# Ten of the 22 column pairs of an FFN's input stage computed as seven block products instead of eight

## The chip, the cores and the metric

The kernel runs on one core of a Trainium2 chip. The core has five engines that work side by side, each through its own queue in order: TensorE (PE in the profile, its weight loads as PEld), VectorE (DVE), ScalarE (ACT), GpSimd (POOL) and SyncE (SP, here a queue for DMAs). They meet by semaphores. The metric is the time of one execution on the device in microseconds (us).

## The reference

One decoder layer over 512 tokens of 1024 channels, in float32. The first half (input projection, attention, pooling mixer, gates, output projection, layer norm) gives `h`. The change concerns the first matrix product of the second half, with `D_FF` = 2816:

```python
a, u = jnp.split(h @ w_ffn_in[l], 2, axis=-1)
a = causal_dwconv(a, conv_w[l], conv_b[l])
f = (jax.nn.gelu(a, approximate=False) * u) @ w_ffn_out[l]
h = layer_norm(ALPHA * h + f, ln2_g[l], ln2_b[l])
```

`w_ffn_in` is 1024 x 5632. The convolution is causal along the tokens, of width 3, channel by channel.

## The kernel before

**Three matmuls for one.** Every float32 operand is split into a high part, rounded to the format fp32r, and a low part, the rest. `split` makes both: ScalarE copies the source into the high part (line 67), VectorE subtracts it from the source (line 68). `mm3` (lines 144 to 148) then issues three matmuls into the same PSUM bank: high x high, high x low, low x high.

**Weights.** `chunks` lists all weight tiles (128 x 1024, 512 KB) in the order of their use. `weights(i)` hands out tile i and has `fetch` load the next ones, up to LEAD = 3 ahead: a DMA on SP's queue into one of three `wraw` buffers, then the split into one of RING = 5 pairs of `whi` and `wlo` buffers. A buffer is filled again when its last reader is done.

**The FFN's input stage.** The 5632 columns are 44 tiles of 128, in 22 pairs: tile 2f is the gate path `a` and tile 2f + 1 the path `u` of the same 128 channels. `hT_hi` and `hT_lo` hold the transposed `h` (8 slices of 128 channels, 512 tokens); `ln1_T` makes them from four token blocks by transposes on TensorE. `fi_mm(j, b, t)` (line 575) computes tile j into a PSUM bank: 8 slices times three matmuls over the tokens `t`. The first five tiles run in two halves of 256 tokens, because the last token blocks come late; the rest run over all 512. After each pair `gated` (line 580) takes the `a` bank through the convolution (one ScalarE and two VectorE instructions), the gelu (ScalarE), and multiplies it with the `u` bank into `fT` (VectorE).

**The output stage** is already a product of 2 x 2 blocks by seven products (`product`, `operands`). Its weight sums are made by DMAs: `tw` is loaded on SP's queue and added to by an accumulating DMA on POOL's queue (lines 641 and 642 for the first product, T3, and line 134 for the later ones). Its token-side operands are differences of `fT`, made by `formed` (line 607) at fixed pairs of the input stage.

**Order.** The program is written stage by stage, and a planner (the tile framework with its schedule on) then decides where each instruction stands in its engine's queue and which free buffer a tile gets. So the loops give what depends on what, and the order on each engine is read from the built program.

Of the kernel before, what the change touches and what calls it, by code (L numbers as in the profile page):

```python
# [22 lines left out]
NF = DFF // P  # L23
# [9 lines left out]
RING = 5  # L33
# [3 lines left out]
NLATE = 4  # L37
KH = NF // 2
TAIL = 8
PRODUCTS = ("T3", "B11", "B21", "T1", "T2", "B22", "T4")  # L40


@with_exitstack
def layer_kernel(ctx: ExitStack, tc: tile.TileContext, xT, x, w_v, w_c, rel_bias, invcnt, w_group,
                 pscale, w_br, w_out, lnr, w_fi, convp, w_fo, out):
    nc = tc.nc
    const = ctx.enter_context(tc.tile_pool(name="const", bufs=1))
    wp = ctx.enter_context(tc.tile_pool(name="wp", bufs=1))
# [7 lines left out]
    def bank(name):  # L56
        return ps.tile([P, S], F32, tag="ps", name=name)
# [5 lines left out]
    def split(hi, lo, src, copy=None):  # L63
        if copy:
            copy(hi, src)
        else:
            nc.scalar.activation(hi, src, AF.Copy)  # L67
        nc.vector.tensor_tensor(lo, src, hi.bitcast(F32), op=ALU.subtract)  # L68
# [9 lines left out]
    chunks = [w_v[c] for c in range(4)]  # L78
# [4 lines left out]
    WO0 = len(chunks)  # L83
    chunks += [w_out[k * P:(k + 1) * P, :] for k in range(KT)]
    FI0 = len(chunks)
    chunks += [w_fi[j] for j in range(2 * NF)]
    FO0 = len(chunks)
    chunks += [(p, c) for p in PRODUCTS for c in range((KH + 1) // 2)]
    ready = {}
    state = {"next": 0, "limit": WO0 - 1}  # L90

    def fetch(pool=None, early=None):
        i = state["next"]
        state["next"] = i + 1
        if isinstance(chunks[i], tuple):
            ready[i] = fetch_fo(i, *chunks[i])
            return
        raw = wp.tile([P, D], F32, tag="wraw", name=f"wraw{i}", bufs=3)
        if pool is None:
            hi = wp.tile([P, D], F32R, tag="whi", name=f"whi{i}", bufs=RING)  # L100
            lo = wp.tile([P, D], F32R, tag="wlo", name=f"wlo{i}", bufs=RING)
        else:
            hi = pool.tile([P, D], F32R, name=f"whi{i}")
            lo = pool.tile([P, D], F32R, name=f"wlo{i}")
        parts = 2 if early else 1
        for c in range(parts):
            sl = slice(c * (D // parts), (c + 1) * (D // parts))
            (nc.scalar if early else nc.sync).dma_start(raw[:, sl], chunks[i][:, sl])
            split(hi[:, sl], lo[:, sl], raw[:, sl], fast if early and c == 0 else None)
            if c == 0 and early:  # L110
                early()
        ready[i] = (hi, lo)

    def half(name, sl):
# [24 lines left out]
    def weights(i):  # L139
        while state["next"] <= min(i + LEAD, state["limit"]):  # L140
            fetch()
        return ready[i]

    def mm3(out_, w, a, start, stop, **kw):
        (wh, wl), (ah, al) = w, a
        nc.tensor.matmul(out_, wh, ah, start=start, stop=False, **kw)  # L146
        nc.tensor.matmul(out_, wh, al, start=False, stop=False, **kw)  # L147
        nc.tensor.matmul(out_, wl, ah, start=False, stop=stop, **kw)  # L148

    def split3(v, a):  # L150
        return tuple(t.rearrange("p (a c) -> p a c", a=a) for t in v)
# [275 lines left out]
    for f in range(KT):  # L427
        if f == KT - LEAD:
            state["limit"] = WO0 + RING - 1
        wh, wl = split3(weights(BR0 + f), KT)  # L430
# [4 lines left out]
        for br in (1, 0):  # L435
            b = bank(f"br{f}_{br}")
# [3 lines left out]
            t = bp.tile([P, S], F32, tag="m", name=f"m{f}_{br}", bufs=4)  # L440
# [19 lines left out]
    lnb = ln_rows(0)  # L460
# [3 lines left out]
    hTp = hp.enter_context(tc.tile_pool(name="hTp", bufs=1, reuse_waits="tile"))  # L464
    hT_hi = hTp.tile([P, KT, S], F32R, name="hT_hi")
    hT_lo = hTp.tile([P, KT, S], F32R, name="hT_lo")
    st = const.tile([P, NT, 4, 6], F32, name="st")
    mv = const.tile([P, NT, 2], F32, name="mv")
    rstd = const.tile([P, NT, 2], F32, name="rstd")
# [67 lines left out]
    def ln1_T(i):  # L537
        for n in range(2):
            b = bank(f"ht{i}_{n}")
            for k in range(4):  # L540
                kt = 4 * n + k
                nc.tensor.transpose(b[:, k * P:(k + 1) * P], xs[:, i, kt * P:(kt + 1) * P], ident)
            split(hT_hi[:, 4 * n:4 * n + 4, i * P:(i + 1) * P], hT_lo[:, 4 * n:4 * n + 4, i * P:(i + 1) * P],
                  b.rearrange("p (a c) -> p a c", a=4))

    def wo_mm(wb, i, k):
        wh, wl = ready[WO0 + k]
# [25 lines left out]
    ln1_vec(3, wb[3])  # L573

    def fi_mm(j, b, t):
        wh, wl = split3(weights(FI0 + j), KT)
# [3 lines left out]
    def gated(j, a, u):  # L580
        y = ytiles[j % 2]
        nc.scalar.activation(y, a, AF.Identity, bias=cvp[:, j, 3:4], scale=cvp[:, j, 2:3])
        nc.vector.scalar_tensor_tensor(y[:, 1:], a[:, :S - 1], cvp[:, j, 1:2], y[:, 1:], op0=ALU.mult, op1=ALU.add)
        nc.vector.scalar_tensor_tensor(y[:, 2:], a[:, :S - 2], cvp[:, j, 0:1], y[:, 2:], op0=ALU.mult, op1=ALU.add)  # L584
        nc.scalar.activation(y, y, AF.Gelu)  # L585
        nc.vector.tensor_tensor(fT[:, j, :], y, u, op=ALU.mult)  # L586

    actp.close()
    fw = ctx.enter_context(tc.tile_pool(name="fw", bufs=1, side="right", reuse_waits="tile"))
    fT = fw.tile([P, NF, S], F32, name="fT")  # L590
    tw = fw.tile([P, KH * S], F32, name="tw")
    sd = [tuple(fw.tile([P, KH, 256], F32R, name=f"sd0_{q}") for q in ("hi", "lo"))]
    rb = fw.tile([P, 3, 256], F32, name="rb")
    NC = (KH + 1) // 2
    cuts = [slice(k, min(k + 4, KH)) for k in range(0, KH, 4)]
    t1, t2 = slice(0, 256), slice(256, 512)
# [10 lines left out]
    def formed(j):  # L607
        for c in cuts:
            if j == c.stop - 1:
                nc.vector.tensor_tensor(rd(c), side(0, c, t1), side(0, c, t2), op=ALU.subtract)  # L610
                side_split(0, c, rd(c))
            if j == KH + c.stop - 1:
                nc.vector.tensor_tensor(side(0, c, t2), side(1, c, t2), side(0, c, t2), op=ALU.subtract)
                nc.vector.scalar_tensor_tensor(rd(c), side(1, c, t2), -1.0, rd(c),
                                               op0=ALU.mult, op1=ALU.subtract)

    hb = {}
    for j in range(RING):
        hb[j] = bank(f"fi{j}")
        fi_mm(j, hb[j], slice(0, 256))  # L620
        if j == 0:
            ln1_T(2)
        elif j == RING - 2:
            ln1_T(3)
    for j in range(RING):
        state["limit"] = FI0 + RING + j
        fi_mm(j, hb[j], slice(256, 512))
        if j % 2:
            gated(j // 2, hb[j - 1], hb[j])
    state["limit"] = len(chunks) - 1  # L630
    ra = hw.tile([P, 8, 256], F32, tag="lnb", name="ra")
    for j in range(RING, 2 * NF):
        hb[j] = bank(f"fi{j}")
        fi_mm(j, hb[j], slice(0, S))
        if j % 2:
            f = j // 2
            gated(f, hb[j - 1], hb[j])
            formed(f)
            if f % 2 == 0 and f >= 6 and f < 6 + 2 * NC:
                c = f // 2 - 3  # L640
                nc.sync.dma_start(tw[:, piece(c)], half("B22", piece(c)))
                nc.gpsimd.dma_start(tw[:, piece(c)], half("B12", piece(c)), accum_op=ALU.add)

    nc.scalar.activation(dummy, cvp[:, 0, :1], AF.Sqrt, bias=eps_t, scale=0.0)
    hp.close()
# [71 lines left out]
    lnb = ln_rows(2)  # L717
# [91 lines left out]
```

## Time and profile before

| | us |
|---|---|
| median of three runs (660.18 to 661.86) | 661.73 |
| the profiled execution | 659.63 |
| its span, first to last instruction | 657.8 |
| TensorE busy | 647.0 |
| VectorE busy | 384.9 |
| ScalarE busy | 284.7 |
| input stage of the FFN, first to last matmul | 301.2 to 543.9 |

The mean granted clock of TensorE is 0.996. A row of a group gives line, engine, operation, what is written from what, shapes and count; then busy time in us and the mean of one in ns; then the engine's idle time before them and what ended it. Matmul durations overlap each other in the trace, so the spacing of their starts is the number to use, not the duration of one.

### The profile page before, as it was taken

What the parts mean: (1) busy time and instruction counts of PE and PEld (TensorE: products, weight loads), DVE (VectorE), ACT (ScalarE), POOL (GpSimd) and SP (SyncE); (2) the same over time, 40 slices, a digit from 0 to 9 for tenths busy, and PEclk for the clock granted to TensorE, in tenths of its full rate; (3) what the DMA queues carried; (4) which work ended last, traced back from release to release, by engine and by line L of the source; (5) the groups of instructions that cost most, each with busy time, mean ns of one, the idle gap of its engine ahead of it and who ended that gap; (6) DMA issues with size and microseconds to landing.
All of it is one profiled execution on the core that took longest, in us unless ns stands there. A gap on an engine that the chain in (4) does not pass through costs nothing.

```text
span 657.8 us, 8016 instructions
## 1 busy us (share of the span) xinstructions
PE 647.0 (98%) x3082; PEld 537.6 (82%) x3082; DVE 384.9 (59%) x560; ACT 284.7 (43%) x393; POOL 95.5 (15%) x139
## 2 busy tenths in 40 slices
PE   8999999999999999999999999999999999999994
PEld 6888787877888888889988888888888888888884
DVE  6466665554532675398455344444534548789596
ACT  6547547585422233132443333333333336555452
POOL 1615351111000124102100000000000001123302
PEclk9999999999999999999999999999999999999998
DMA  8643222212222228209942222232222334979905
GB/s 319 213 145 97 81 83 77 97 64 70 92 96 97 96 97 305 79 1 302 255 146 97 97 96 97 96 99 99 95 96 100 96 99 107 219 180 190 283 4 128
DMA packets 24918, 83.70 MB, mean 127 GB/s; under 512 B 3240, under 2 KB 3496, under 8 KB 24624
## 3 DMA queue, kind: packets, MB, share of 16 engines
q1 hardware_dynamic: 19024, 63.24, 27.6%
q0 software_dynamic: 5280, 18.90, 13.3%
q10 hardware_dynamic: 576, 1.05, 0.5%
q8 instruction: 24, 0.39, 0.2%
q14 instruction: 14, 0.11, 0.1%
HBM read 80.01 MB, written 3.17 MB: 126 GB/s over the span
## 4 chain that ended last, share of the span: by engine, by line
PE 94%; DVE 2%; POOL 2%; ACT 1%; DMA 1%; issue 0%; DVEq 0%; ACTq 0%; POOLq 0%
PE fi L148 12%; PE fi L147 12%; PE fi L146 12%; PE g L146 4%; PE g L148 4%; PE g L147 4%; PE v L247 3%; PE wo L147 2%; PE br L148 2%; PE br L147 2%; PE wo L148 2%; PE wo L146 2%; PE br L146 2%; PE fod L148 2%; PE foa L148 2%; PE foa L147 2%
## 5 line engine op out<-in xcount | busy, mean ns | idle before, releaser
L68 DVE TENSOR_TENSOR wlo<-wraw,whi 128x1024 fp32r<-128x1024 f32 (+1 forms) x105 | 134.6, 1286 | 116.0 <-ACT whi L67 114.2
L67 ACT ACTIVATE whi<-wraw 128x1024 fp32r<-128x1024 f32 (+1 forms) x104 | 108.8, 1048 | 183.7 <-PE fi L147 83.6
L147 PE MATMUL fi<-hT_lo,whi 128*128 128x512 f32 (+1 forms) x392 | 143.8, 367 | 0.0
L148 PE MATMUL fi<-hT_hi,wlo 128*128 128x512 f32 (+1 forms) x392 | 143.8, 367 | 0.0
L146 PE MATMUL fi<-hT_hi,whi 128*128 128x512 f32 (+1 forms) x392 | 143.5, 368 | 0.0
L147 PEld LDWEIGHTS fi<-hT_lo,whi 128*128 128x128 f32 x392 | 73.9, 189 | 12.2
L148 PEld LDWEIGHTS fi<-hT_hi,wlo 128*128 128x128 f32 x392 | 73.9, 189 | 12.1
L146 PEld LDWEIGHTS fi<-hT_hi,whi 128*128 128x128 f32 x392 | 73.6, 189 | 12.1
L134 POOL DMA_DIRECT2D tw<-in_w_fo x18 | 15.8, 913 | 267.2 <-DVE wlo L68 267.2
L146 PE MATMUL g<-xT_hi,whi 128*128 128x512 f32 x128 | 50.3, 393 | 0.0
L148 PE MATMUL g<-xT_hi,wlo 128*128 128x512 f32 x128 | 49.9, 390 | 0.0
L147 PE MATMUL g<-xT_lo,whi 128*128 128x512 f32 x128 | 49.8, 389 | 0.0
L67 ACT ACTIVATE whi<-tw 128x1024 fp32r<-128x1024 f32 (+1 forms) x30 | 29.5, 985 | 25.0 <-PE fi L147 11.3
L586 DVE TENSOR_TENSOR fT<-y,fi 128x512 f32<-128x512 f32 x22 | 15.1, 688 | 40.3 <-PE fi L148 39.6
L68 DVE TENSOR_TENSOR wlo<-tw,whi 128x1024 fp32r<-128x1024 f32 (+1 forms) x30 | 33.4, 1131 | 8.4 <-ACT whi L67 8.3
L585 ACT ACTIVATE y<-y 128x512 f32<-128x512 f32 x22 | 13.9, 633 | 43.1 <-DVE y L584 43.1
L148 PEld LDWEIGHTS g<-xT_hi,wlo 128*128 128x128 f32 x128 | 24.0, 188 | 5.1
L146 PEld LDWEIGHTS g<-xT_hi,whi 128*128 128x128 f32 x128 | 24.0, 188 | 5.0 <-issue 0.2
L147 PEld LDWEIGHTS g<-xT_lo,whi 128*128 128x128 f32 x128 | 24.1, 188 | 4.9
L352 POOL TENSOR_SCALAR pp<-pp,rs 128x128 f32<-128x128 f32 (+3 forms) x32 | 21.8, 698 | 37.5 <-PE g L148 18.3
L444 POOL TENSOR_TENSOR mt<-m,m 128x512 f32<-128x512 f32 x8 | 11.2, 1394 | 96.0 <-DVE m L441 79.3
L146 PE MATMUL wo<-whi,mx_hi 128*128 128x512 f32 x64 | 25.0, 390 | 0.0
(204 smaller groups left out, 1185.6 us busy)
## 6 DMA issues: line engine op xcount, KB each, us to landing
wraw<-in_w_fi SPq DMA_DIRECT2D x44, 512.0 KB, 3.3
wraw<-in_w_c SPq DMA_DIRECT2D x28, 512.0 KB, 3.3
tw<-in_w_fo POOLq DMA_DIRECT2D x20, 512.0 KB, 7.3
tw<-in_w_fo SPq DMA_DIRECT2D x10, 512.0 KB, 3.6
wraw<-in_w_fo SPq DMA_DIRECT2D x10, 512.0 KB, 3.5
wraw<-in_w_br SPq DMA_DIRECT2D x8, 512.0 KB, 3.2
wraw<-in_w_out SPq DMA_DIRECT2D x8, 512.0 KB, 3.2
strip<-F_d POOLq DMA_DIRECT2D x8, 256.0 KB, 3.6
```

What stands on the lines that cost most here:

```text
L67: nc.scalar.activation(hi, src, AF.Copy)
L68: nc.vector.tensor_tensor(lo, src, hi.bitcast(F32), op=ALU.subtract)
L134: nc.gpsimd.dma_start(raw, half(then[1:], sl), accum_op=ALU.add)
L146: nc.tensor.matmul(out_, wh, ah, start=start, stop=False, **kw)
L147: nc.tensor.matmul(out_, wh, al, start=False, stop=False, **kw)
L148: nc.tensor.matmul(out_, wl, ah, start=False, stop=stop, **kw)
L247: nc.tensor.matmul(bs[j], xs_[j][a], (wh, wl)[b], start=kt == 0 and n == 0, stop=False)
L352: nc.gpsimd.tensor_scalar(pp[:, offs[i]:offs[i] + n], pp[:, offs[i]:offs[i] + n], rs[:, i:i + 1], 1.0, op0=ALU.mult, op1=ALU.mult)
L444: nc.gpsimd.tensor_tensor(mt, m[1], m[0], op=ALU.add)
L585: nc.scalar.activation(y, y, AF.Gelu)
L586: nc.vector.tensor_tensor(fT[:, j, :], y, u, op=ALU.mult)
```

## The change

Ten pairs (4, 5, 7, 8, 10, 11, 13, 14, 16, 17, the list `SEVEN`) are computed as one 2 x 2 block product: the weights in blocks by column tile (`a`, `u`) and by half of the 1024 channels (1, 2), `h` in blocks by half of the channels and half of the tokens. Eight block products of 4 slices x 256 tokens become seven, each of 4 x 3 matmuls of 256 columns. The weights of such a pair are four tiles: A = [a1, a2] as loaded; D = u2, half a tile, as loaded; X = [a1 + u1, u1 + u2], made by a load on SP's queue and an accumulating DMA on POOL's queue (`fetch_sums`, into two buffers of their own); Y = [a1 + u1 + u2, a1 + a2 + u1 + u2], made from A and X by two additions of VectorE (`fetch_seven`). On the token side four differences of blocks of `h` (nT1, T3, nT2, T4) are made and split once (`t_form`), from a float32 copy `hraw` that `ln1_T` now stores as well.

`seven(f)` issues six of the seven products and leaves the seventh, with `gated`, in `pending`: it is issued inside the next pair. Four products go on adding into one half bank (`chain`), whose value is read between them: ScalarE copies it three times out of PSUM (with `low` once), VectorE adds three times. The sign of `u` comes out reversed, and the last multiplication takes it back.

The buffers of the output stage (`tw`, `sd`, `rb`, `ra`) are opened only after pair 17, where the sums' and differences' buffers are closed. So the loads of T3 into `tw` and the differences of `fT`, which `formed` spread over pairs 3 to 21, are now written in the last four pairs.

```diff
+SEVEN = (4, 5, 7, 8, 10, 11, 13, 14, 16, 17)
+AHEAD = 5
...
     def fetch(pool=None, early=None):
         i = state["next"]
         state["next"] = i + 1
+        while sums and xu and fi_at[sums[0], "X"] <= i + AHEAD:
+            fetch_sums(sums.pop(0))
         if isinstance(chunks[i], tuple):
-            ready[i] = fetch_fo(i, *chunks[i])
+            ready[i] = (fetch_fo if i >= FO0 else fetch_seven)(i, *chunks[i])
             return
...
+    def fetch_sums(f):
+        x_ = raws[f, "X"] = xu.tile([P, D], F32, tag="xraw", name=f"xraw{f}", bufs=2)
+        a, u = w_fi[2 * f], w_fi[2 * f + 1]
+        v = x_.rearrange("p (a c) -> p a c", a=2)
+        (pst, pn), (est, _) = u.ap
+        nc.sync.dma_start(v, bass.AP(tensor=u.tensor, offset=u.offset, ap=[[pst, pn], [0, 2], [est, S]]))
+        nc.gpsimd.dma_start(v, bass.AP(tensor=a.tensor, offset=a.offset,
+                                       ap=[[pst, pn], [u.offset + S - a.offset, 2], [est, S]]), accum_op=ALU.add)
+
+    def fetch_seven(i, f, q):
+        n = S if q == "D" else D
+        if q == "X":
+            raw = raws[f, "X"]
+        else:
+            raw = raws[f, q] = wp.tile([P, D], F32, tag="wraw", name=f"wraw{i}", bufs=3)[:, :n]
+        if q == "Y":
+            a, x_ = raws[f, "A"], raws[f, "X"]
+            for c, o in ((slice(0, S), x_[:, S:]), (slice(S, D), raw[:, :S])):
+                nc.vector.tensor_tensor(raw[:, c], o, a[:, c], op=ALU.add)
+        elif q != "X":
+            nc.sync.dma_start(raw, w_fi[2 * f] if q == "A" else w_fi[2 * f + 1][:, S:])
...
+        split(hi, lo, raw)
+        return hi, lo
...
+            nc.scalar.activation(hraw[:, 4 * n:4 * n + 4, i * P:(i + 1) * P], b, AF.Copy)
...
+    def t_form(n):
+        b11, b12, b21, b22 = (hraw[:, k, t] for k in (k1, k2) for t in (t1, t2))
+        if n in ("nT1", "T3"):
+            v, a = {"nT1": (b11, b11), "T3": (b12, b22)}[n]
+            nc.vector.tensor_tensor(v, a, b12, op=ALU.subtract)
+        else:
+            v, a = {"nT2": (b22, b11), "T4": (b21, b22)}[n]
+            nc.vector.scalar_tensor_tensor(v, a, -1.0, v, op0=ALU.mult, op1=ALU.subtract)
+        split(*tt[n], v)
...
+    def s_mm(f, q, part, act_, b, start, skip=True):
+        wh, wl = split3(weights(fi_at[f, q]), 4 if q == "D" else KT)
+        for k in range(4):
+            mm3(b, (wh[:, 4 * part + k, :], wl[:, 4 * part + k, :]), (act_[0][:, k, :], act_[1][:, k, :]),
+                start and k == 0, k == 3, skip_group_check=not start)
...
+    def seven(f):
+        ba, bb, bc = (bank(f"s{q}{f}") for q in "abc")
+        chain, low, c11 = ba[:, 256:], bb[:, :256], bc[:, :256]
+        y = ytiles[f % 2]
+        u = xu.tile([P, S], F32, tag="u", name=f"u{f}", bufs=2)
+        s_mm(f, "A", 0, whole(k1, t1), chain, True)
+        nc.scalar.activation(y[:, t1], chain, AF.Copy)
+        s_mm(f, "X", 0, tt["T3"], low, True)
+        nc.scalar.activation(u[:, t2], low, AF.Copy)
+        if pending:
+            pending.pop()()
+        s_mm(f, "Y", 0, tt["nT2"], chain, False)
+        nc.scalar.activation(u[:, t1], chain, AF.Copy)
+        s_mm(f, "A", 1, whole(k2, t1), c11, True)
+        s_mm(f, "D", 0, tt["T4"], low, False)
+        nc.vector.tensor_tensor(u[:, t1], u[:, t1], low, op=ALU.add)
+        s_mm(f, "X", 1, tt["nT1"], chain, False)
+        nc.vector.tensor_tensor(u[:, t2], u[:, t2], chain, op=ALU.add)
+        nc.vector.tensor_tensor(ba[:, t1], y[:, t1], c11, op=ALU.add)
+
+        def close():
+            s_mm(f, "Y", 1, whole(k2, t2), chain, False)
+            gated(f, ba, u, -1.0)
+
+        pending.append(close)
...
+            if pending:
+                pending.pop()()
+                xus.close()
+                spp.close()
...
+            elif pieces:
+                c = piece(pieces.pop(0))
+                nc.sync.dma_start(tw[:, c], half("B22", c))
+                nc.gpsimd.dma_start(tw[:, c], half("B12", c), accum_op=ALU.add)
```

More of the change, by code (lines that the diff above doesn't have):

```diff
@@ L85, in layer_kernel @@
     FI0 = len(chunks)
-    chunks += [w_fi[j] for j in range(2 * NF)]
+    fi_at = {}
+    for f in range(NF):
+        for q in "AXDY" if f in SEVEN else "au":
+            fi_at[f, q] = len(chunks)
+            chunks.append((f, q) if f in SEVEN else w_fi[2 * f + "au".index(q)])
     FO0 = len(chunks)
@@ L112, in fetch @@
         ready[i] = (hi, lo)
+    raws = {}
+    sums = list(SEVEN)
+    xu = None
+    def fetch_sums(f):
[18 more added lines that the diff above has]
+            nc.sync.dma_start(raw, w_fi[2 * f] if q == "A" else w_fi[2 * f + 1][:, S:])
+        hi = wp.tile([P, D], F32R, tag="whi", name=f"whi{i}", bufs=RING)[:, :n]
+        lo = wp.tile([P, D], F32R, tag="wlo", name=f"wlo{i}", bufs=RING)[:, :n]
+        split(hi, lo, raw)
+        return hi, lo
     def half(name, sl):
@@ L585, in gated @@
         nc.scalar.activation(y, y, AF.Gelu)
[L586 to L596, printed above, removed]
+        if sign:
+            nc.vector.scalar_tensor_tensor(fT[:, j, :], y, sign, u, op0=ALU.mult, op1=ALU.mult)
+        else:
+            nc.vector.tensor_tensor(fT[:, j, :], y, u, op=ALU.mult)
     def side(kh, c, t):
@@ L605, in rd @@
         return rb if c.start == 8 else ra[:, c, :]
[L607 to L615, printed above, removed]
+    actp.close()
+    fw = ctx.enter_context(tc.tile_pool(name="fw", bufs=1, side="right", reuse_waits="tile"))
+    fT = fw.tile([P, NF, S], F32, name="fT")
+    spp = ExitStack()
+    sp = spp.enter_context(tc.tile_pool(name="sp", bufs=1, side="right", reuse_waits="tile"))
+    tt = {n: tuple(sp.tile([P, 4, 256], F32R, name=f"{n}_{q}") for q in ("hi", "lo"))
+          for n in ("nT1", "T3", "nT2", "T4")}
+    sp.tile([P, 48], F32, name="sp_gap")
+    NC = (KH + 1) // 2
+    cuts = [slice(k, min(k + 4, KH)) for k in range(0, KH, 4)]
+    t1, t2 = slice(0, 256), slice(256, 512)
+    k1, k2 = slice(0, 4), slice(4, 8)
     hb = {}
@@ L619, in layer_kernel @@
         hb[j] = bank(f"fi{j}")
[L620 removed]
+        fi_mm(j, hb[j], t1)
         if j == 0:
@@ L626, in layer_kernel @@
         state["limit"] = FI0 + RING + j
-        fi_mm(j, hb[j], slice(256, 512))
+        fi_mm(j, hb[j], t2)
         if j % 2:
             gated(j // 2, hb[j - 1], hb[j])
+    for n in ("nT1", "T3", "nT2", "T4"):
+        t_form(n)
     state["limit"] = len(chunks) - 1
[L631 to L642, printed above, removed]
+    pending = []
@@ new lines, in layer_kernel @@
+    hr.close()
+    xus = ExitStack()
+    xu = xus.enter_context(tc.tile_pool(name="xu", bufs=1, reuse_waits="tile"))
+    last = max(SEVEN)
+    for f in range(RING // 2, last + 1):
+        if f in SEVEN:
+            seven(f)
+            continue
+        for j in range(max(RING, 2 * f), 2 * f + 2):
+            hb[j] = bank(f"fi{j}")
+            fi_mm(j, hb[j], slice(0, S))
+            if pending:
+                pending.pop()()
+        gated(f, hb[2 * f], hb[2 * f + 1])
+    spread = []
@@ new lines, in layer_kernel @@
+    for f in range(last + 1, NF):
+        for j in range(2 * f, 2 * f + 2):
+            hb[j] = bank(f"fi{j}")
+            fi_mm(j, hb[j], slice(0, S))
+            if pending:
+                pending.pop()()
+                xus.close()
+                spp.close()
+                sq = ctx.enter_context(tc.tile_pool(name="sq", bufs=1, side="right", reuse_waits="tile"))
+                tw = sq.tile([P, KH * S], F32, name="tw")
+                sd = [tuple(sq.tile([P, KH, 256], F32R, name=f"sd0_{q}") for q in ("hi", "lo"))]
+                rb = sq.tile([P, 3, 256], F32, name="rb")
+                ra = hw.tile([P, 8, 256], F32, tag="lnb", name="ra")
+                pieces = list(range(NC))
+                early = list(cuts)
+            elif pieces:
+                c = piece(pieces.pop(0))
+                nc.sync.dma_start(tw[:, c], half("B22", c))
+                nc.gpsimd.dma_start(tw[:, c], half("B12", c), accum_op=ALU.add)
+        gated(f, hb[2 * f], hb[2 * f + 1])
+        if early:
+            c = early.pop(0)
+            nc.vector.tensor_tensor(rd(c), side(0, c, t1), side(0, c, t2), op=ALU.subtract)
+            side_split(0, c, rd(c))
+            spread.append(c)
+        for c in list(spread):
+            if f >= KH + c.stop - 1 and (f > last + 1):
+                spread.remove(c)
+                nc.vector.tensor_tensor(side(0, c, t2), side(1, c, t2), side(0, c, t2), op=ALU.subtract)
+                nc.vector.scalar_tensor_tensor(rd(c), side(1, c, t2), -1.0, rd(c),
+                                               op0=ALU.mult, op1=ALU.subtract)
@@ L644, in layer_kernel @@
+    assert not pieces and not early and not spread
     nc.scalar.activation(dummy, cvp[:, 0, :1], AF.Sqrt, bias=eps_t, scale=0.0)
```

13 lines of the change are left out of this document (9 added, 4 removed).

## The prediction

> **What bounds the kernel now.** I read the page's busy shares, the chain that ended last, the waits of TensorE, then tables by stretch and groups by shape inside the FFN's input stage, the only stage whose arithmetic changes.
>
> ```profile
> span 657.8 us, 8016 instructions
> PE 647.0 (98%) x3082; PEld 537.6 (82%) x3082; DVE 384.9 (59%) x560; ACT 284.7 (43%) x393; POOL 95.5 (15%) x139
> PE 94%; DVE 2%; POOL 2%; ACT 1%; DMA 1%; issue 0%; DVEq 0%; ACTq 0%; POOLq 0%
> PE warm_ps L176 <- DVE warm L173: 1.2, 1, 1.2
> PE zb L146 <- ACT difh L67: 0.5, 2, 0.3
> PE v L247 <- ACT whi L158: 0.5, 1, 0.5
> ```
>
> TensorE is busy for 98% of the span, carries 94% of the chain, and its three waits come to 2.2 us, none in the stage. So the time of this stage is the number of matmuls times their spacing, as long as the other engines keep up. The stretch tables give the spacing (first all instructions, then those touching the stage's banks alone; after the length come PE, PEld, DVE, ACT, in the first also POOL, then clock, DMA share and GB/s):
>
> ```profile
> 317.50:331.90 14.40, 14.40 (x121) 14.40 (x121) 7.49 (x9) 7.73 (x9) 0.88 (x1) 1.00 0.99 255
> 331.90:348.20 16.30, 16.30 (x73) 13.47 (x73) 8.61 (x10) 6.00 (x9) 0.00 (x0) 1.00 0.39 129
> 500.00:543.90 43.90, 43.90 (x195) 36.38 (x194) 20.38 (x22) 13.72 (x17) 0.00 (x0) 1.00 0.31 96
> 543.90:559.00 15.10, 15.10 (x68) 12.51 (x67) 13.76 (x14) 10.52 (x12) 2.22 (x3) 1.00 0.41 90
> ```
>
> ```profile
> 331.90:543.90 212.00, 212.00 (x936) 175.39 (x935) 43.63 (x60) 15.26 (x20) 1.00 0.29 100
> ```
>
> From 331.9 to 543.9 stand 936 matmuls of 512 columns: 212.00 / 936 = 0.2265 us each. From 317.5 to 331.9 the first five tiles get their second 256 columns: 14.40 / 121 = 0.119 us each. A half-width matmul costs 0.525 of a full one, not 0.5; on that the change rests. Single rows show a little more:
>
> ```profile
> 317.81 0.28 PE L146 MATMUL fi<-hT_hi,whi 128*128 128x256 f32 x1
> 317.82 0.19 PEld L147 LDWEIGHTS fi<-hT_lo,whi 128*128 128x128 f32 x1
> 317.94 0.28 PE L147 MATMUL fi<-hT_lo,whi 128*128 128x256 f32 x1
> 317.94 0.19 PEld L148 LDWEIGHTS fi<-hT_hi,wlo 128*128 128x128 f32 x1
> ...
> 319.98 0.28 PE L146 MATMUL fi<-hT_hi,whi 128*128 128x256 f32 x1
> ```
>
> From 317.81 to 319.98 are 18 steps, 0.1206 us each: my upper bound of the spacing. A load lasts 0.19 us and the next starts 0.12 us later, beside the matmul before.
>
> **The change, part by part.** *TensorE.* A pair costs 2 tiles x 8 k x 3 = 48 matmuls of 512 columns now, 48 x 0.2265 = 10.87 us. As seven products it is 7 x 4 x 3 = 84 of 256 columns: 84 x 0.119 = 10.00 us (10.13 at 0.1206). Saved: 0.87 us a pair (0.74), 8.7 us for ten (7.4). All of it lies on the path.
>
> The Trainium skill, TensorE: Matmul & The Clock Gate, section "Back-to-back issue gap", gives N / 2.4 + 2.5 ns between warm matmuls. Estimated from that page a pair would go from 10.36 to 9.17 us, and ten would save 11.9 us. The trace shows 119 and 226.5 ns where the page gives 109 and 216, so my sum stays with the rows.
>
> *VectorE, ScalarE in a pair.* The durations:
>
> ```profile
> L68 DVE TENSOR_TENSOR wlo<-wraw,whi 128x1024 fp32r<-128x1024 f32 x101 | 132.0, 1309 | 116.0 <-ACT whi L67 114.2 <-PE tr L366 0.3
> L68 DVE TENSOR_TENSOR wlo<-wraw,whi 128x512 fp32r<-128x512 f32 x4 | 2.8, 688 | 0.0
> L687 DVE TENSOR_TENSOR xs<-xs,fo_cut 128x256 f32<-128x256 f32 x2 | 0.8, 413 | 0.5 <-PE fo_cut L148 0.5
> L583 DVE SCALAR_TENSOR_TENSOR y<-fi,cvp,y 128x511 f32<-128x511 f32 x22 | 16.4, 744 | 0.0
> L584 DVE SCALAR_TENSOR_TENSOR y<-fi,cvp,y 128x510 f32<-128x510 f32 x22 | 16.5, 750 | 0.8
> L586 DVE TENSOR_TENSOR fT<-y,fi 128x512 f32<-128x512 f32 x22 | 15.1, 688 | 40.3 <-PE fi L148 39.6 <-ACT y L585 0.7
> L67 ACT ACTIVATE whi<-wraw 128x1024 fp32r<-128x1024 f32 x101 | 106.9, 1060 | 182.6 <-PE fi L147 83.6 <-PE g L147 23.6 <-issue 22.1
> L158 ACT ACTIVATE whi<-wraw 128x320 fp32r<-128x320 f32 x1 | 0.5, 471 | 1.6 <-DMA wraw<-in_w_v 1.6
> L582 ACT ACTIVATE y<-fi,cvp 128x512 f32<-128x512 f32 x22 | 16.8, 763 | 0.0
> L585 ACT ACTIVATE y<-y 128x512 f32<-128x512 f32 x22 | 13.9, 633 | 43.1 <-DVE y L584 43.1
> ```
>
> An ordinary pair asks VectorE for 2 x 1.309 + 0.744 + 0.750 + 0.688 = 4.80 us. A seven-product pair asks for three full low parts and a half one (3 x 1.309 + 0.688 = 4.62), two half adds that make Y (1.38), three adds of 256 columns out of PSUM (1.24) and the same 2.18: 9.42 us in a 10.00 us pair. The pattern is two such pairs to one ordinary: 2 x 9.42 + 4.80 = 23.6 us of 30.9, 76%. ScalarE: 3 x 1.060, a half one (0.688 as bound), three copies of 256 columns at 0.471 (the 320-column row is nearest), 0.763 and 0.633: 6.7 us; a period 2 x 6.7 + 3.5 = 16.9, 55%. Neither is a bound by its sum; VectorE ran at 13.76 of 15.10 us (91%) from 543.9 to 559.0 without TensorE stopping. I cost this work at nothing while matmuls cover it. What can show is order, since every engine works in order. In the built order of the changed kernel I looked for two kinds of place:
> - The high and low part of a new weight tile need 1.060 + 1.309 = 2.37 us after a slot comes free. For Y of pair 8 the last reader of its slot is A's second half; 22 half matmuls later the high part is wanted, 14 later still the low part: 36 x 0.119 = 4.3 us. 1.9 us is left, more than one 1.309 us split in the way.
> - The closing product waits for two adds behind the sixth (2 x 0.413 = 0.83 us). At nine of ten pairs 22 or more matmuls lie between (2.6 us or more); at pair 10 only ten, 1.19 us, so 0.36 us is left, and a split in the way costs up to 0.95 us.
>
> For all waits I take 1.0 us, near the end that these covers give; the ends are 0 and one split per pair, 13.1 us.
>
> *Before the first such pair.* Eight copies of the transposed tiles (ScalarE), four differences, four splits:
>
> ```profile
> L67 ACT ACTIVATE hT_hi<-ht 128x512 fp32r<-128x512 f32 x8 | 4.2, 600 | 16.0 <-PE ht L542 16.0
> L610 DVE TENSOR_TENSOR ra<-fT 128x1024 f32<-128x1024 f32 x2 | 2.5, 1226 | 0.1
> L68 DVE TENSOR_TENSOR sd_lo<-fT,sd_hi 128x1024 fp32r<-128x1024 f32 x8 | 9.7, 1223 | 6.5 <-ACT sd_hi L67 6.5
> ```
>
> VectorE: 4 x 1.226 + 4 x 1.223 = 9.8 us, with Y's adds (1.4) and about one low part more 12.5 us, on top of 7.49 + 8.61 = 16.1 us busy in the 30.7 us before 348.2, where pair 4 begins: 28.6 of 30.7. ScalarE gets 8 x 0.600 + 4 x 1.060 = 9.0 on 13.7. Cover is thin, but the first wanted is T3, second of four formed. Nothing; if the cover goes, some 2 us.
>
> *DMA, with SP's and POOL's queues.*
>
> ```profile
> q1 hardware_dynamic: 19024, 63.24, 27.6%
> q0 software_dynamic: 5280, 18.90, 13.3%
> wraw<-in_w_fi SPq DMA_DIRECT2D x44, 512.0 KB, 3.3
> tw<-in_w_fo POOLq DMA_DIRECT2D x20, 512.0 KB, 7.3
> tw<-in_w_fo SPq DMA_DIRECT2D x10, 512.0 KB, 3.6
> DMA to landing us min/median/max: 5.3/7.8/14.1
> ```
>
> q1 moved 63.24 MB in 27.6% of 657.8 us, 1.5 us per 512 KB; the accumulating q0 takes 2.4 us. A seven-product pair moves A, half a tile D, and X twice (once accumulating): 1.5 + 0.8 + 1.5 + 2.4 = 6.2 us in 10.00, a period 15.4 of 30.9. X is complete 3.3 + 7.3 = 10.6 us after SP issues it; POOL has nothing else in this stage, but on SP the loads of A and D stand behind X's wait for its slot. Two X slots serve two pairs per 30.9 us, so even the longest landing (14.1) fits. Nothing.
>
> *Hand-over to the output stage.* T3's buffer is now loaded and added to in the last four pairs: 5.5 pieces x 3.9 = 21.5 us on 0.31 x 43.9 = 13.6: 35 of 43.9. A piece needs 3.6 + 7.3 = 10.9 us (17.7 at the longest) and some 35 us remain. The token-side differences come together there too: about 9 us of VectorE on 20.38 of 43.9. Nothing.
>
> *Sum.* The profiled execution took 659.63 us (span 657.8, 1.83 around it): 659.63 - 8.7 + 1.0 = 651.9. The median of the runs shown, 661.73, is 0.3% above it; that difference, 2 us, is also about what a measurement here can tell from no change.
>
> **Rivals.**
> - *Some waits.* A 1.309 us split stands in the way once in each of the five groups of two: 6.5 us for my 1.0, 657.4. For it: VectorE at 94% within a seven-product pair. Against: the covers above.
> - *Slower: VectorE holds the closing product.* A split in front of it at every one of ten pairs, 13.1 us against 8.7: 664.0. It decides from 0.87 us a pair. For it: three of VectorE's adds wait on PSUM and all stand in one queue with the splits. Against: 2.6 us of cover at nine places.
> - *Weight loads bind.* If loads could not overlap, 84 x 0.19 = 16.0 us a pair would replace 10.87: 711. A spacing of 10.87 / 84 = 0.1294 already ends the gain. The Trainium skill, TensorE: Matmul & The Clock Gate, "The mechanism" of the part on packing, says that loads overlap running matmuls only where the row group differs, which here it does not. The trace disagrees: 121 loads of 0.19 us in 14.40 us. Open is only whether that lasts for 20 us instead of 14.
> - *The gain is given back.* T3 lands late, the first product waits: up to 8 us, 659.6. For it: 80% DMA load. Against: 35 us of time for an 11 us transfer.
>
> **How the numbers follow.** Forecast 0.64 (651.9, own range 650 to 655); some waits 0.14; slower by VectorE 0.12; loads bind 0.03; given back 0.07. Faster than 657.7: the forecast and two thirds of the first rival, 0.74; same: the rest of it and most of the last, 0.10; slower 0.16. The range runs from 649.5 (no wait, small gains at the edges) to 661, past the first and last rivals; about 0.15 above and 0.04 below stay out.
>
> **What would show it.** Right: 840 half matmuls at 0.119 to 0.121 us, the stage's last matmul near 536, no PE wait over 1 us, VectorE near 76% from pair 4 to 17. Wrong: PE waiting on VectorE's adds or low parts inside the pairs; spacing above 0.125 in blocks without a wait; the first output matmul late behind T3's splits. The forecast falls if waits come to more than 0.67 us a pair.

## The result, and the profile after

The changed kernel takes 652.46 us at the median, beside 661.74 us for the kernel before in the same comparison: a ratio of 0.9869, with a 95% interval of 0.9846 to 0.9892. That is 9.3 us less; the forecast was 651.9. The profiled execution of the changed kernel took 652.89 us, 6.7 below the profiled one of before, which had been the fastest of its runs.

The page of the changed kernel: span, busy time of each engine, shares of the chain.

```profile
span 651.2 us, 8945 instructions
PE 639.8 (98%) x3442; PEld 548.0 (84%) x3442; DVE 432.7 (66%) x638; ACT 318.1 (49%) x455; POOL 106.9 (16%) x149
PE 91%; DVE 3%; DMA 2%; ACT 1%; POOL 1%; issue 1%; DVEq 0%; ACTq 0%; POOLq 0%
```

With 360 matmuls more, many of them half as wide, TensorE is busy for 7.2 us less, and VectorE works 47.8 us more. TensorE's waits, the whole list (total, count, longest):

```profile
PE warm_ps L214 <- DVE warm L211: 1.2, 1, 1.2
PE zb L184 <- ACT difh L69: 0.5, 2, 0.3
PE v L285 <- DVE whi L193: 0.4, 1, 0.4
PE fod L185 <- DVE wlo L70: 0.3, 1, 0.3
```

The first three were there before, none in the input stage: none of the waits that the prediction looked for came. The fourth, new, is in the output stage.

TensorE's rows by tile (min/median/max ns, first and last start). The stage begins with the first `fi` matmul and ends with the first `foe` matmul:

```profile
L184 PE MATMUL fi<-hT_hi,whi x232: 277/389/403, 302.1 to 535.5; 128*128 128x512 f32 x76, 128*128 128x256 f32 x40
L186 PE MATMUL fi<-hT_hi,wlo x232: 278/389/402, 302.4 to 536.0; 128*128 128x512 f32 x76, 128*128 128x256 f32 x40
L184 PE MATMUL sa<-hT_hi,whi x80: 277/283/340, 349.0 to 501.6; 128*128 128x256 f32 x80
L184 PE MATMUL foe<-whi,sd_hi x33: 388/390/396, 536.2 to 636.0; 128*128 128x512 f32 x33
```

From 302.1 to 536.2 are 234.1 us; before, from 301.2 to 543.9, it was 242.7. The stage gained 8.6 us, 0.86 a pair. By stretches (length, busy time of PE, PEld, VectorE, ScalarE, GpSimd, clock, DMA share, GB/s):

```profile
317.90:332.50 14.60, 14.60 (x124) 14.60 (x123) 14.50 (x15) 10.70 (x11) 0.00 (x0) 1.00 0.29 85
332.50:349.00 16.50, 16.50 (x75) 13.70 (x74) 9.47 (x13) 5.94 (x9) 3.17 (x3) 1.00 0.73 179
349.00:380.00 31.00, 31.00 (x218) 29.02 (x217) 21.55 (x28) 15.70 (x23) 2.98 (x3) 1.00 0.59 154
380.00:411.00 31.00, 31.00 (x219) 29.06 (x218) 22.87 (x32) 15.74 (x23) 2.41 (x2) 1.00 0.58 153
411.00:442.00 31.00, 31.00 (x219) 29.05 (x218) 21.20 (x30) 14.43 (x21) 2.41 (x2) 1.00 0.57 153
442.00:473.00 31.00, 31.00 (x220) 29.06 (x219) 23.08 (x32) 16.68 (x24) 1.20 (x1) 1.00 0.52 136
504.00:536.20 32.20, 32.20 (x144) 26.69 (x143) 22.38 (x26) 12.52 (x15) 5.20 (x6) 1.00 0.95 263
```

The first row is the head: VectorE has 14.50 of 14.60 us to do, and TensorE does not stop. In the middle, a period of two seven-product pairs and an ordinary one, VectorE is busy for 21.2 to 23.1 of 31 us and ScalarE for 14.4 to 16.7. The last row is the hand-over, with the DMA engines 95% busy.

### The profile page after: what moved, and what is told of

Same layout as the page of the kernel before. It is cut to its first block, busy times and chain, and to the rows that moved or that the text cites. A ratio compares the mean times of both kernels' runs of the same rounds, so it can differ in the third digit from the quotient of the medians.

```text
span 651.2 us, 8945 instructions
## 1 busy us (share of the span) xinstructions
PE 639.8 (98%) x3442; PEld 548.0 (84%) x3442; DVE 432.7 (66%) x638; ACT 318.1 (49%) x455; POOL 106.9 (16%) x149
## 4 chain that ended last, share of the span: by engine, by line
PE 91%; DVE 3%; DMA 2%; ACT 1%; POOL 1%; issue 1%; DVEq 0%; ACTq 0%; POOLq 0%
PE fi L184 7%; PE fi L186 7%; PE fi L185 7%; PE g L184 5%; PE g L186 4%; PE g L185 4%; PE v L285 3%; PE sa L186 3%; PE sa L184 3%; PE sa L185 3%; PE wo L186 2%; PE br L186 2%; PE wo L185 2%; PE br L185 2%; PE wo L184 2%; PE br L184 2%
## 5 line engine op out<-in xcount | busy, mean ns | idle before, releaser
L70 DVE TENSOR_TENSOR wlo<-wraw,whi 128x1024 fp32r<-128x1024 f32 (+1 forms) x115 | 141.4, 1232 | 69.9 <-ACT whi L69 68.6
L69 ACT ACTIVATE whi<-wraw 128x1024 fp32r<-128x1024 f32 (+1 forms) x114 | 114.6, 1009 | 129.7 <-PE g L185 23.7
L186 PE MATMUL fi<-hT_hi,wlo 128*128 128x512 f32 (+1 forms) x232 | 81.8, 353 | 0.0
L185 PE MATMUL fi<-hT_lo,whi 128*128 128x512 f32 (+1 forms) x232 | 81.8, 353 | 0.0
L184 PE MATMUL fi<-hT_hi,whi 128*128 128x512 f32 (+1 forms) x232 | 81.5, 354 | 0.0
L186 PEld LDWEIGHTS fi<-hT_hi,wlo 128*128 128x128 f32 x232 | 43.9, 189 | 5.8
L185 PEld LDWEIGHTS fi<-hT_lo,whi 128*128 128x128 f32 x232 | 43.9, 189 | 5.6
L184 PEld LDWEIGHTS fi<-hT_hi,whi 128*128 128x128 f32 x232 | 43.6, 189 | 5.4
L132 POOL DMA_DIRECT2D xraw<-in_w_fi x10 | 12.2, 1220 | 176.2 <-DMA xraw<-in_w_fi 91.9
L186 PE MATMUL wo<-whi,mx_lo 128*128 128x512 f32 x64 | 24.9, 390 | 0.0
```

The costliest lines, as they stand in the source:

```text
L132: nc.gpsimd.dma_start(v, bass.AP(tensor=a.tensor, offset=a.offset, ap=[[pst, pn], [u.offset + S - a.offset, 2], [est, S]]), accum_op=ALU.add)
```

## Experiments: how much each pair gives

The first series changes only which pairs are done as seven products, in one line:

```diff
-SEVEN = (4, 5, 7, 8, 10, 11, 13, 14, 16, 17)
+SEVEN = (17,)                                          # e_one
+SEVEN = (5, 8, 11, 14, 17)                             # e_five
+SEVEN = (4, 5, 6, 8, 9, 10, 12, 13, 14, 16, 17)        # e_eleven
+SEVEN = (4, 5, 6, 7, 9, 10, 11, 12, 14, 15, 16, 17)    # e_twelve
+SEVEN = tuple(range(4, 18))                            # e_fourteen
```

> One pair (17) as seven products, everything around it as in the changed kernel: the float32 copies, the four differences, and the hand-over to the output stage in the last four pairs. Cover theory (each pair gives 0.87 us, the rest is hidden): 0.9 us below the kernel before, that is no measurable change, and the stage itself 0.9 us shorter. Fixed-cost rival (the work around the pairs, head and hand-over, costs 1 to 2 us however many pairs there are; the profiled changed kernel lost 0.9 us ahead of the stage and 1.1 us behind it): 0 to 1 us above the kernel before.

> Five pairs (5, 8, 11, 14, 17), none next to another. Cover theory, linear in the pairs: 5 x 0.87 = 4.4 us below the kernel before. Fixed-cost rival with 1 us paid once: 3.4 below. If the second pair of each group of two carried waits, five single pairs would give more than half of what ten gave (9.3 us at the medians): above 5.

> The changed kernel once more, beside the others of this call. If the saving is 0.87 us a pair less what the work around the pairs costs (0 to 1 us): 7.7 to 8.7 us below the kernel before, against 9.3 at the medians so far; the stage from first to last matmul 234 us as in the first profile. If the 0.9 us lost ahead of the stage in the first profile belongs to that execution, the v stage ends at 24.0 or at 25.0 here without regard to the kernel.

> Eleven pairs, three groups of three (4 to 6, 8 to 10, 12 to 14) and one of two (16, 17). If a row of three still runs without a stop: the stage 0.87 us shorter than with ten, 233.1 us, 9.6 below the kernel before. If it is the third pair of a row that brings the stops seen in rows of four and of fourteen (0.3 to 1.2 us each, a high part of ScalarE late): the stage 234 to 236 us, level with the changed kernel or 2 us above it.

> Twelve pairs in groups of four (4 to 7, 9 to 12, 14 to 17) with one ordinary pair between. VectorE 4 x 9.42 + 4.8 = 42.5 of 50.9 us, 83%. If one ordinary pair in five is enough to catch up: 1.7 us below the changed kernel, 10.4 below the kernel before, no stop of TensorE. If the stops of fourteen come from the length of the row: level with the changed kernel, with one or two stops of about 1 us in the third or fourth pair of a group.

> Fourteen pairs in a row, 4 to 17, no ordinary pair between. Cover theory: 14 x 0.87 = 12.2 us below the kernel before, 3.5 below the changed kernel, VectorE near 94% in the stage, no wait of TensorE. VectorE rival: at 9.42 us of work in a 10.00 us pair and no ordinary pair to catch up in, every upset of the order is a wait; the four additional pairs give nothing or take something back, so 8 us below the kernel before or less, with waits of TensorE on VectorE's splits or adds inside the pairs.

What was measured. The medians stand against the kernel before in the same comparison; the stage runs from the first `fi` to the first `foe` matmul of each profile and was 242.7 us before.

| pairs as seven products | median less that of before, us | ratio (95%) | stage, us | stage less before, us |
|---|---|---|---|---|
| 1 | -1.1 | 0.9985 (0.9972 to 0.9997) | 241.9 | -0.8 |
| 5, single | -3.9 | 0.9929 (0.9913 to 0.9945) | 238.7 | -4.0 |
| 10, twos (the change) | -9.3 | 0.9869 (0.9846 to 0.9892) | 234.1 | -8.6 |
| 10, measured again | -9.0 | 0.9863 (0.9845 to 0.9880) | 234.0 | -8.7 |
| 11, threes | -6.0 | 0.9907 (0.9893 to 0.9920) | 236.7 | -6.0 |
| 12, fours | -6.3 | 0.9899 (0.9882 to 0.9917) | 235.9 | -6.8 |
| 14 in a row | -9.8 | 0.9843 (0.9825 to 0.9861) | 234.1 | -8.6 |

The rows behind the stage lengths, for one pair, for five and for fourteen:

```profile
L184 PE MATMUL fi<-hT_hi,whi x376: 277/389/402, 303.5 to 544.7; 128*128 128x512 f32 x148, 128*128 128x256 f32 x40
L184 PE MATMUL foe<-whi,sd_hi x33: 389/389/396, 545.4 to 644.5; 128*128 128x512 f32 x33
```

```profile
L184 PE MATMUL fi<-hT_hi,whi x312: 277/389/403, 302.2 to 540.2; 128*128 128x512 f32 x116, 128*128 128x256 f32 x40
L184 PE MATMUL foe<-whi,sd_hi x33: 389/390/397, 540.9 to 640.0; 128*128 128x512 f32 x33
```

```profile
L184 PE MATMUL fi<-hT_hi,whi x168: 278/388/398, 301.1 to 534.5; 128*128 128x512 f32 x88, 128*128 128x256 f32 x80
L184 PE MATMUL foe<-whi,sd_hi x33: 388/389/397, 535.2 to 634.3; 128*128 128x512 f32 x33
PE sa L184 <- ACT whi L69: 2.2, 2, 1.2
```

What follows. Up to ten pairs the stage is linear in them: 0.8, 0.8 and 0.87 us a pair for one, five and ten. One pair alone, with all the copies, differences and late loads around it, is already 1.1 us faster (0.2 to 1.8 by the interval), and its stage is 0.8 us shorter, so that work is hidden; the fixed-cost rival falls. Beyond two in a row the gain ends. Fourteen pairs should have shortened the stage by 12.2 us and shortened it by 8.6: 3.6 us went into stops, of which the list names the two longest, 2.2 us, both on a high part of ScalarE. With twelve and eleven the stage is longer than with ten. In the time of the whole kernel eleven is slower than ten clear of both intervals; the interval of twelve overlaps that of one of the two measurements of ten. The waits:

```profile
PE sb L184 <- ACT whi L69: 2.2, 2, 1.1
```

```profile
PE fi L186 <- DVE wlo L70: 1.1, 2, 0.5
PE fi L184 <- ACT whi L69: 0.4, 2, 0.2
```

(the first of twelve pairs, the other two of eleven). My first case for twelve, drawn from VectorE's load alone, was wrong. The second had the two stops right but not the time: 10.4 us less were due and 6.8 came, so the stage is 1.8 us longer than with ten and not level with it. Eleven lost even more than its second case allowed (236.7 us for 234 to 236). The first stop with twelve pairs ends at 425.7, in a stretch from 411 to 442 where VectorE is busy for 21.77 of 31 us, within the range of ten pairs. ScalarE's timeline up to that stop (start, duration, instruction, idle before):

```profile
420.27 1.06 ACT L69 ACTIVATE whi<-wraw 128x1024 fp32r<-128x1024 f32 x1 [2.72 <-PE sa L185]
421.24 0.76 ACT L623 ACTIVATE y<-sa,cvp 128x512 f32<-128x512 f32 x1
423.05 1.06 ACT L69 ACTIVATE whi<-wraw 128x1024 fp32r<-128x1024 f32 x1 [1.05 <-issue]
424.01 0.76 ACT L623 ACTIVATE y<-sa,cvp 128x512 f32<-128x512 f32 x1
424.68 1.04 ACT L69 ACTIVATE whi<-xraw 128x1024 fp32r<-128x1024 f32 x1
```

The awaited split is the last line, X of pair 12. It stands behind the split of A of the same pair, and that one idled first. In the built program A's split waits for a slot of the ring of five whose last reader is the closing product of pair 10. So the chain is closing product, slot, A, X, in ScalarE's order, at 70% load of VectorE. VectorE has no idle time in the 3.4 us around the stop, but until 421.37 it had sat idle for 2.51 us, waiting for a high part of ScalarE: the order bunches its work too. X's own slot was not free much earlier: in the built program its last reader is the second half of A of pair 11, whose last matmul starts at 423.64; by an estimate from these two starts (423.64 and 424.68) X could have been at most about 1 us earlier with nothing of ScalarE's in front of it.

The stops of eleven pairs show the same chain without X. At the first of them, the first tile of the ordinary pair 11 has the slot of Y of pair 9, whose closing product has its last matmul at 412.41. Its high part follows on ScalarE, again after idle time, and its low part on VectorE right behind, done at 414.98, and the matmul that waits for the low part starts at 415.03:

```profile
412.66 1.06 ACT L69 ACTIVATE whi<-wraw 128x1024 fp32r<-128x1024 f32 x1 [1.05 <-issue]
413.75 1.22 DVE L70 TENSOR_TENSOR wlo<-wraw,whi 128x1024 fp32r<-128x1024 f32 x1
```

From the start of the high part to the end of the low part are 2.3 us, the 2.37 us of the prediction's first kind of place. With three pairs in a row that cover is gone.

## Experiments: half-width matmuls alone

`e_halves` is the kernel before with the same ten pairs run in two halves of tokens.

```diff
-        fi_mm(j, hb[j], slice(0, S))
+        if j // 2 in HALVES:                # the ten pairs of SEVEN
+            fi_mm(j, hb[j], t1)
+            fi_mm(j, hb[j], t2)
+        else:
+            fi_mm(j, hb[j], slice(0, S))
```

> The kernel before with the same ten pairs as ordinary tiles, but each tile run over 256 tokens first and the other 256 after: 96 matmuls of 256 columns a pair for 48 of 512, nothing else changed. By the spacings (0.119 and 0.2265 us): 11.42 for 10.87 us a pair, 5.5 us above the kernel before. The changed kernel should then lie ten times 12 x 0.119 = 14.3 us below this one. If weight loads bound at half width when it lasts longer than 14 us: 96 x 0.19 = 18.2 us a pair, 74 above.

It took 666.99 us against 660.24, a ratio of 1.0092 (1.0075 to 1.0109). Its rows:

```profile
L147 PE MATMUL fi<-hT_hi,whi x552: 278/284/397, 302.1 to 550.6; 128*128 128x256 f32 x133, 128*128 128x512 f32 x51
L147 PE MATMUL foe<-whi,sd_hi x33: 388/390/397, 551.3 to 650.4; 128*128 128x512 f32 x33
```

The stage is 249.2 us, 6.5 more than before where 5.5 was expected. From 10 x (96 s - 10.87) = 6.5 the spacing s of a half matmul is 0.120 us, between the 0.119 and the 0.1206 of the prediction. So the change is two parts of opposite sign: halving costs 6.5 us, and dropping one product in eight gives 249.2 - 234.0 = 15.2. Weight loads did not become the bound over 10 x 11.5 us of such work, so the rival that they bind falls.

## Experiments: what covers VectorE's work

`e_close_now` writes the seventh product at the end of its own pair.

```diff
-        pending.append(close)
+        close()
+        pending.append(lambda: None)
```

> The changed kernel with the seventh product written at the end of its own pair instead of inside the next one. Cover theory (the 22 matmuls between are what hides VectorE's two adds and the splits in front of them): at least 10 x 0.85 = 8.5 us above the changed kernel, up to 10 x (0.85 + 1.31) = 21.6 with one split in the way each time, so no gain left over the kernel before; waits of TensorE on VectorE's adds at every pair. Rival (the adds are early enough, or the order comes out the same anyway): within 1 us of the changed kernel.

It took 651.42 us, a ratio of 0.9858 (0.9844 to 0.9873), level with the changed kernel (651.83 in the same comparison). Its stage is 234.0 us:

```profile
L184 PE MATMUL fi<-hT_hi,whi x232: 277/389/402, 301.1 to 534.4; 128*128 128x512 f32 x76, 128*128 128x256 f32 x40
L184 PE MATMUL foe<-whi,sd_hi x33: 388/389/396, 535.1 to 634.3; 128*128 128x512 f32 x33
```

The rival holds: the built order of TensorE puts other products in front of the closing one in either case, and the two orders differ at a few places only. This run therefore did not take the cover away, and says nothing on what it is worth.

`e_load2` and `e_load4` write two or four more multiplications for VectorE into each of the ten pairs.

```diff
+    extra = xu.tile([P, D], F32, name="extra")
...
+        for _ in range(2):                  # 4 in e_load4
+            nc.vector.tensor_tensor(extra, extra, extra, op=ALU.mult)
         s_mm(f, "A", 1, whole(k2, t1), c11, True)
```

> The changed kernel with four more multiplications of 128x1024 on VectorE in each of the ten pairs, on a buffer that nothing else reads (1.22 us each by the row of that shape): 9.42 + 4.9 = 14.3 us of VectorE in a 10.0 us pair, 33.4 in a 30.9 us period. If VectorE's budget is that of the period: about 2.5 us each for five periods, 10 to 15 above the changed kernel. If it is that of the pair, because ordinary pairs can't catch up: up to 4.3 a pair, 43 above.

> The changed kernel with two more multiplications of 128x1024 on VectorE in each of the ten pairs (four of them cost 14 us): 9.42 + 2.45 = 11.9 us of VectorE in a 10.0 us pair, 28.5 in a 30.9 us period (92%). Period budget: 0 to 2 us above the changed kernel. Pair budget (no catching up in the ordinary pair): 1.9 us a pair, about 19 above; with covers of 2 us for each group of two, about 9.

With four, 665.69 us, 13.9 above the changed kernel of the same comparison, which is inside the 10 to 15 of the period's budget. With two, 657.40 us, a ratio of 0.9964 (0.9950 to 0.9977); the stage is 240.1 us, 6.1 more than the changed kernel's, and that is neither of the two bounds. But the multiplications did not run where they were written (with two, then with four; min/median/max ns, first and last start):

```profile
L707 DVE TENSOR_TENSOR extra<-extra x20: 1212/1218/1224, 334.4 to 397.8; 128x1024 f32<-128x1024 f32 x20
L707 DVE TENSOR_TENSOR extra<-extra x40: 1217/1224/1234, 334.2 to 454.3; 128x1024 f32<-128x1024 f32 x40
```

Nothing but these multiplications reads `extra`, so the planner was free to place them early. All twenty were over at 399, all forty at 455.5, about one every 3 us in both runs, and none came after. So neither run puts its load on each pair, and that four of them met the forecast for a period's budget is luck. The stretches and TensorE's waits with two:

```profile
349.00:380.00 31.00, 30.51 (x213) 28.24 (x213) 29.59 (x37) 14.04 (x20) 1.21 (x1) 1.00 0.51 139
380.00:411.00 31.00, 28.30 (x192) 26.07 (x191) 26.91 (x33) 12.17 (x18) 2.41 (x2) 0.94 0.55 143
411.00:442.00 31.00, 31.00 (x216) 28.92 (x215) 25.05 (x34) 17.34 (x25) 2.41 (x2) 1.00 0.63 166
```

```profile
PE sa L184 <- ACT y L699: 2.0, 1, 2.0
PE sa L186 <- DVE wlo L70: 0.7, 2, 0.5
```

All of the loss lies before 411, and so does all of the added work. In the first 31 us ten of the multiplications start, 12.2 us of work, where VectorE had 9.45 of 31 us free in the changed kernel; it is now busy for 29.59, and TensorE begins to stop. The row from 411 on holds none of them. So the runs show that twelve more microseconds in the first period are too much for these covers; how much VectorE has to spare in a pair, early or late, stays open.

## Experiments: the stops of fourteen in a row

`e_fourteen_ring` gives the half tile D a buffer of its own, so that A no longer gets the slot of Y of the pair before last. It is one buffer, so each D now waits for the product with the D before it. `e_fourteen_pool` moves Y's two additions to GpSimd.

```diff
+        if q == "D":                        # e_fourteen_ring
+            hi = xu.tile([P, S], F32R, tag="dhi", name=f"whi{i}")
+            lo = xu.tile([P, S], F32R, tag="dlo", name=f"wlo{i}")
...
-                nc.vector.tensor_tensor(raw[:, c], o, a[:, c], op=ALU.add)
+                nc.gpsimd.tensor_tensor(raw[:, c], o, a[:, c], op=ALU.add)    # e_fourteen_pool
```

> The fourteen pairs in a row, with the high and low part of the half tile D in a buffer of their own instead of in the ring of five. Ring theory (in a row of seven-product pairs A's split of the next pair waits for the slot of Y, whose last reader is the deferred closing product; that made the two stops of 1.2 and 1.0 us and the smaller ones, 4.1 us in all above the spacing): the stops go, 3 to 4 us below the fourteen without it, 12 to 13 below the kernel before. VectorE theory (85 to 90% busy is the limit, whatever the slots): within 1 us of the fourteen, the waits moved to low parts or adds.

> Fourteen pairs in a row with Y's two additions on GpSimd instead of VectorE: 1.38 us less for VectorE in each 10.0 us pair (8.0, 80%), about 2 x 1.3 us more for GpSimd. VectorE theory (its load makes the stops of fourteen): the stops go, 3 to 4 us below fourteen, about 13 below the kernel before. Rival (it is the order and the latency of splits, not the load): within 1 us of fourteen, or above it by the longer additions and by the waits of GpSimd's queue, where each accumulating load waits up to 17 us for the load ahead of it.

Both were slower than fourteen without them. With the ring changed, 657.38 us (0.9948, 0.9931 to 0.9965) and a stage of 240.4: the stops moved to other splits and came together, and twice the clock fell behind them (last section). With the additions on GpSimd, 655.26 us (0.9917, 0.9902 to 0.9933) and a stage of 237.4. VectorE was not relieved: from 349 to 536 it is busy for 148.62 us, with the additions on its own queue 148.44 (to 535.2). The groups by shape between 349 and 500 say why; the low part of X with the additions on VectorE, then with them on GpSimd, and GpSimd's additions themselves:

```profile
L70 DVE TENSOR_TENSOR wlo<-xraw,whi 128x1024 fp32r<-128x1024 f32 x13 | 15.9, 1221 | 0.8 <-ACT whi L69 0.7
```

```profile
L70 DVE TENSOR_TENSOR wlo<-xraw,whi 128x1024 fp32r<-128x1024 f32 x13 | 29.5, 2271 | 1.7 <-ACT whi L69 1.7
L144 POOL TENSOR_TENSOR wraw<-wraw,wraw 128x512 f32<-128x512 f32 x13 | 28.1, 2163 | 1.0
L144 POOL TENSOR_TENSOR wraw<-xraw,wraw 128x512 f32<-128x512 f32 x13 | 22.2, 1707 | 8.5 <-DVE wlo L70 7.7 <-DMA wraw<-in_w_fi 0.6
```

So neither run settles what sets the limit beyond two in a row. For twelve and eleven pairs the chain through the slot is seen; taking that dependency out of the fourteen moved the whole order, and other stops came. Whether an order exists that runs fourteen pairs without stops stays open. Fourteen pairs (0.9843) and ten (0.9863) can't be told apart by their intervals, so no version here is known to beat the change.

## Why the prediction was right, point by point

- *The spacing, 8.7 us.* Right: 8.6 and 8.7 in two profiles, 0.8 for one pair, 4.0 for five, and 0.120 us for a half matmul by itself. By the estimate from the Trainium skill, TensorE: Matmul & The Clock Gate, section "Back-to-back issue gap", ten pairs would have saved 11.9 us; the stage disagrees with it by 3 us, and the rows of before were the better source.
- *Waits, 1.0 us.* Mis-sized: the changed kernel has none in the stage. The two places that the prediction named held, Y of pair 8 and the closing product of pair 10, so the end at 0 is what came. The first kind of place, a slot that comes free late, is where the stops of eleven and twelve pairs came.
- *VectorE and ScalarE at nothing.* Right, with 21.2 to 23.1 of 31 us measured for 76% (23.6) forecast. Two durations were off, both on the safe side: a low part takes 1.22 us in this stage, not the 1.309 of the mean over the whole kernel, and a copy of 256 columns out of PSUM takes ScalarE 0.38 us, not 0.471.

```profile
L705 ACT ACTIVATE u<-sa 128x256 f32<-128x256 f32 x10 | 3.8, 382 | 5.2 <-PE sa L186 5.2
L710 DVE TENSOR_TENSOR u<-u,sa 128x256 f32<-128x256 f32 x10 | 4.2, 419 | 10.1 <-PE sa L186 10.0
```

- *The head, nothing.* Right. VectorE is full from 317.9 to 332.5, but it has caught up before pair 4 begins: it sits idle for 4.09 us until X of pair 4 has landed. Up to 349 it is busy for 24.0 us, where the prediction counted 28.6.

```profile
341.05 0.69 DVE L144 TENSOR_TENSOR wraw<-xraw,wraw 128x512 f32<-128x512 f32 x1 [4.09 <-DMA xraw<-in_w_fi]
```

- *DMA, nothing.* Right. X's accumulating load lands in 5.8 us at the median, for the 7.3 allowed (KB each, median us to landing), and no wait of TensorE in the stage leads to a transfer.

```profile
xraw<-in_w_fi POOLq DMA_DIRECT2D x10, 512.0 KB, 5.8
```

- *The hand-over, nothing.* Right to 0.3 us, the wait of `fod`. The DMA engines were busier than forecast, 95% for 80%, and the first output matmul still follows the last input one by 0.2 us. The rival that gives the gain back here falls; one pair alone, with the same hand-over, shows no cost.
- *VectorE holds the closing product.* Not in the change. With eleven to fourteen pairs the gain does end, but on high and low parts that come late in order more than on the adds.
- *The sum.* That the median, 652.46, lies 0.6 us from the forecast is in part luck. The sum started from the fastest run of before, 2.1 us below the median, and forecast a gain of 7.7 us, where the medians show 9.3 and the stage 8.6. The profiled execution took 652.89, 1.0 above the forecast, with 1.0 us fewer waits; 2.0 us came from outside the stage. 0.9 of it stands before the stage: the last v matmul of its own loop (line 285, line 247 before) starts at 24.8, at 23.8 before. Over the profiles of all these kernels, whose first 300 us are the same work but for the copies, that time lies between 23.6 and 26.1 (26.1 with one pair, 23.9 with ten measured again), so it belongs to the execution. The other 1.1 lies in the output stage and the tail; from the last output matmul to the end of the span it was 8.5 to 9.5 us in these profiles, 8.8 before.

## What to carry to other kernels

A product saved is worth its matmuls times the spacing of the width they will then have, read from the same kernel's own rows; here 6.5 of the 15.2 us went back into the narrower width. Work added to engines beside TensorE was free at up to 75% of VectorE's time with an ordinary pair in between to catch up, and cost stops at a load no higher once a ring slot tied a tile's first split to the last product of the pair before last. When more of a good change gives less, look at order and slots before load. When a run adds work to find what an engine can spare, find in its trace where that work ran before reading its time: what nothing waits for, the planner may put elsewhere. And do not count on GpSimd to relieve VectorE; in this kernel it took back what it gave.

## What was not expected of the hardware

*The clock falls after a few short stops.* With the ring changed, no single wait of TensorE in the stage was over 0.9 us:

```profile
PE sa L190 <- DVE wlo L70: 1.8, 2, 0.9
PE sb L188 <- ACT whi L69: 1.7, 3, 0.8
PE sa L188 <- ACT y L703: 0.9, 1, 0.9
```

```profile
390.80:394.20 3.40, 1.98 (x13) 1.37 (x12) 3.40 (x7) 1.35 (x2) 0.00 (x0) 1.00 0.89 142
394.30:397.70 3.40, 3.40 (x19) 3.40 (x18) 2.57 (x4) 0.63 (x1) 0.00 (x0) 0.52 0.26 74
```

TensorE was busy for 1.98 of 3.40 us, and in the next 3.4 us its granted clock was 0.52: half matmuls 0.213 us apart for 0.119, some 16 of them, 1.5 us lost again. It happened twice in that run (again at 459), twice with four additional multiplications and once with two, where the clock column of 380 to 411 above shows it as 0.94. With twelve pairs, TensorE was busy for 2.05 of 3.40 us around the first stop, and the clock stayed:

```profile
422.50:425.90 3.40, 2.05 (x15) 1.64 (x15) 3.40 (x6) 2.85 (x4) 1.05 (x1) 1.00 0.46 60
```

With four additional multiplications it stayed once beside 1.98 of 3.40 us too, so the edge lies near there and not at one value. The Trainium skill, TensorE: Matmul & The Clock Gate, section "Why this matters for your kernels", warns of gaps of more than about 3 us. The half clock and its 3.4 us agree with the window that the same page gives (section "What's actually happening"). The length of 3 us does not: here the clock fell after short stops that together left TensorE idle for 1.4 us in 3.4.

*GpSimd and VectorE slow each other down.* The rows above: VectorE's subtraction of 128x1024 from 1.22 to 2.27 us, and an addition of 128x512 on GpSimd 1.7 to 2.2 us, where GpSimd's eight operations of that shape earlier in the same run (`mt`) take 1.39. VectorE's multiply-add on a PSUM bank (line 624) stays at 0.74 us, also where a GpSimd addition runs all through it. The Trainium skill, GPSIMD Engine Reference, section "Specifications", says that GpSimd's path to SBUF is shared with VectorE, with contention where VectorE reads two SBUF inputs. This trace agrees, by a factor of 1.86.
